# A two-layer hybrid block on one core: the rest of both layers' modulation on TensorE within the first mixers, instead of on GpSimd and ScalarE during the dense feed-forward

## The chip, the cores and the metric

The kernel runs on one core of one Trainium2 chip. The metric is device time in microseconds from the first to the last instruction of an execution, as the median of several runs. TensorE is called PE, its weight loads PEld, VectorE DVE, ScalarE ACT, GpSimd POOL; SP is the engine whose queue issues the transfers of this kernel.

## The reference

Two layers work on 256 latent and 256 context tokens of width 1024. Each layer first makes its modulation: six vectors of 1024 (shift, scale and gate for the mixers and for the feed-forward), once from the conditioning vector `c` and once from `c_ctx`. The two columns of silu(c) are multiplied with a 1024 x 6144 matrix per layer.

```python
for l in range(DEPTH):
    mod_lat = (jax.nn.silu(c) @ ada_w[l] + ada_b[l])[:, None, :]
    mod_ctx = (jax.nn.silu(c_ctx) @ ada_w[l] + ada_b[l])[None, None, :]
    sh_m, sc_m, g_m, sh_f, sc_f, g_f = jnp.split(mod_lat, N_MOD, axis=-1)
    hx = modulate(rmsnorm(x, norm_mix_g[l]), sh_m, sc_m)
    yx, _, _ = mix(l, hx @ w_in[l], True, hf_c[:, -1], hb_c[:, 0])
    x = x + g_m * yx
    hxf = modulate(rmsnorm(x, norm_ffn_g[l]), sh_f, sc_f)
    x = x + g_f * channel_mix(l, hxf)
```

`mix` splits the input projection into Fourier, Hyena and S5 heads and joins them with an output projection. `channel_mix` is a dense SwiGLU of width 2816 in the first layer and eight SwiGLU experts (two per token) in the second. The context tokens run through the first layer in the same way and through the second as far as the S5 states.

## The kernel before, in words

All operands are 32-bit; the large matmuls split each weight tile into a high part (`wh`, L189 on ScalarE) and a rest (`wl`, L190 on VectorE) and do three products (`mm3`). The kernel runs in stages: the start (modulation needed first, the norm, the Hyena filter and the S5 parameters of layer one), `mixers(0, ...)` (input projection in 14 tiles, S5 in six groups of four heads' groups, Hyena, Fourier), the output projection with residual and norm (L1156, L512 to L541), the dense feed-forward (gate and up into `pgu`, down into `pacc`, L1214 the residual), `mixers(1, ...)`, the router, and the experts, which stream 336 MB of weights.

The modulation has 48 columns of 128 per layer, kept in `mods[l]`; twelve chunks of four columns each. It is made in three ways. `ada_pe` (start, layer one's chunks 0 to 3) and `ada_ring` (chunks 4 to 7) use TensorE: a chunk's weights come as 512-wide rows, eight matmuls with the two columns of silu(c) as stationary operand write four strips of 32 partitions of one PSUM tile `pad`, ScalarE copies it to `adr`, four small matmuls with `sum4` add the strips up and transpose them, and ScalarE copies the result to `mods`. `ada_ring` reads a chunk in four transfers of 512 KB into a ring of two buffers `ar`. The third way is `ada` (L427): each of the other 64 columns comes transposed (`adaT`), and for each of the two vectors either VectorE multiplies and sums at once (L435, 8 times) or GpSimd multiplies with `crow`, a copy of silu(c) on all partitions (L438), and ScalarE sums (L439), 88 times. Columns 32 to 47 of layer one are made around the output projection, the 48 of layer two in `ahead(fi)`, eight per round of the feed-forward, with the layer's S5 matrices (`mats1`). `mods_done` adds the bias (L382) and makes the scale `Gm` (L385). `crow` itself is made at the start by 16 matmuls into `pcr`.

`fill0(q)` is called by `mixers` after S5 group q (0 to 5) and once at its end (6); it places the ring chunks. A scheduler orders the instructions of each engine; each engine then executes its own list strictly in that order, SP's list of transfers too, and waits on semaphores.

Of the kernel before, what the change touches and what calls it, by code (L numbers as in the profile page):

```python
# [8 lines left out]
F32 = mybir.dt.float32  # L9
# [71 lines left out]
def _prep(i):  # L81
# [6 lines left out]
    a['adaN'] = cc(i['ada_w'][0].reshape(KD, 128, 12, 512).transpose(2, 1, 0, 3))  # L88
    a['adaT'] = cc(i['ada_w'].transpose(0, 2, 1).reshape(2, 48, 128, D))
# [44 lines left out]
def build(tc, A, out, dbg=None, upto='all'):  # L134
# [71 lines left out]
    crow = par.tile([128, 2, D], F32, name="crow")  # L206
# [182 lines left out]
    def ada_pe(c, pool, cnt=[0]):  # L389
        pa = pt_('acc', (128, 512), "pad")  # L390
        for kh in range(2):
            cnt[0] += 1
            if cnt[0] % 2 or pool is None:
                r = load(A['adaN'][c][:, 4 * kh:4 * kh + 4], 4, 512)
            else:
                r = pool.tile([128, 4, 512], F32, name="raw2", tag="raw2", bufs=2)
                SP.dma_start(r, A['adaN'][c][:, 4 * kh:4 * kh + 4])
            for k in range(4):
                mm(pa[32 * k:32 * k + 32], scol32[:, 8 * kh + 2 * k:8 * kh + 2 * k + 32], r[:, k], kh == 0, kh == 1)
        row = (pool or wraw).tile([128, 512], F32, name="adr", tag="adr" if pool else "raw", bufs=1 if pool else 2)  # L400
        act(row, pa, AF.Copy)
        pt = pa[:, 0:8].rearrange("p (j s) -> p j s", s=2)
        for j in range(4):
            mm(pt[:, j], row[:, 128 * j:128 * j + 128], sum4, j == 0, j == 3, skip_group_check=True)
        act(mods[0][:, 4 * c:4 * c + 4], pt, AF.Copy)
        mods_done(0, 4 * c, 4)


    def ada_ring(c, pool):
        pa = pt_('acc', (128, 512), "pad")  # L410
        for j in range(4):
            r = pool.tile([128, 2, 512], F32, name="ar", tag="ar", bufs=2)
            SP.dma_start(r, A['adaN'][c][:, 2 * j:2 * j + 2])
            for i in range(2):
                k = 2 * j + i
                b = 32 * (k % 4)
                mm(pa[b:b + 32], scol32[:, 2 * k:2 * k + 32], r[:, i], j < 2, j > 1)
        row = pool.tile([128, 512], F32, name="adr", tag="ar", bufs=2)
        act(row, pa, AF.Copy)
        pt = pa[:, 0:8].rearrange("p (j s) -> p j s", s=2)  # L420
        for j in range(4):
            mm(pt[:, j], row[:, 128 * j:128 * j + 128], sum4, j == 0, j == 3, skip_group_check=True)
        act(mods[0][:, 4 * c:4 * c + 4], pt, AF.Copy)
        mods_done(0, 4 * c, 4)


    def ada(l, m0, m1, eng, pool):  # L427
        for m in range(m0, m1):
            r = pool.tile([128, D], F32, name="ar", tag="ar", bufs=2)
            SP.dma_start(r, A['adaT'][l, m])  # L430
            for s in range(1 if l == 1 and m >= 16 else 0, 2):
                o = mods[l][:, m, s:s + 1]
                if eng(m, s) == 'v':
                    jk = par.tile([128, D], mybir.dt.bfloat16, name="jk", tag="jk", bufs=1)
                    stt(jk, r, 1.0, crow[:, s], op0=mul, op1=mul, accum_out=o)  # L435
                else:
                    pd = par.tile([128, D], F32, name="pd", tag="pd", bufs=1)
                    gtt(pd, r, crow[:, s], op=mul)  # L438
                    act(pd, pd, AF.Copy, accum_out=o)  # L439
            if m % 8 == 7:  # L440
                mods_done(l, m - 7, 8, 1 if l == 1 and m >= 16 else 0)
# [108 lines left out]
    def s5_mats(p, l, q, M, rh, rd):  # L550
# [25 lines left out]
        for i, (src, op) in enumerate(((bre, sub), (bim, add))):  # L576
            tt_(src, bt(PB[0]), bh(bb[:, i]), op=mul)
            (tt_ if l else gtt)(x2, bt(PB[1]), bh(bb[:, 1 - i]), op=mul)
# [503 lines left out]
    with tc.tile_pool(name="filt", bufs=1) as p_:  # L1082
# [7 lines left out]
        with tc.tile_pool(name="prm", bufs=1) as p2_, tc.tile_pool(name="start", bufs=1) as st, banks(f=3, fk=1):  # L1090
# [3 lines left out]
            for s in range(2):  # L1094
                for h in range(2):
                    pb = paux((128, 4, 128), "pcr")
                    for k in range(4):
                        mm(pb[:, k], scol[:, 4 * h + k, s:s + 1].to_broadcast([128, 128]), ident, True, True)
                    act(crow[:, s, 512 * h:512 * h + 512], pb.rearrange("p a b -> p (a b)"), AF.Copy)
# [14 lines left out]
    with z_es:  # L1114
# [3 lines left out]
        with tc.tile_pool(name="z0p", bufs=1) as z2, tc.tile_pool(name="ada0", bufs=1) as p_:  # L1118
            def fill0(q):
                if q == 0:  # L1120
                    ada_ring(4, p_)
                if q == 1:
                    ada_ring(5, p_)
                if q == 3:
                    ada_ring(6, p_)
                if q == 4:
                    ada_ring(7, p_)
            mixers(0, hH, hL, z2, yH, yL, fill0)
# [13 lines left out]
        ada(0, 32, 36, lambda m, s: 'gv'[s], apl)  # L1142
        ada(0, 36, 40, lambda m, s: 'gv'[s], apl)
        ada(0, 40, 44, lambda m, s: 'gg'[s], apl)
        ada(0, 44, 48, lambda m, s: 'gg'[s], apl)
# [41 lines left out]
    with tc.tile_pool(name="ffn", bufs=2, side="right") as fp, banks(gu=3, fk=1):  # L1187
# [42 lines left out]
        def ahead(fi):  # L1230
            ada(1, 8 * fi, 8 * fi + 8, lambda m, s: 'g', apl)
            for q in MATS1[fi]:
                mats1(q)
# [584 lines left out]
```

## Time and profile before

| | |
|---|---|
| median of 3 runs | 1851.45 us (1850.5 to 1854.9) |
| profiled execution | 1846.75 us, its span 1844.9 us |
| PE busy | 1708.1 us (93%) |
| DVE, ACT, POOL busy | 824.4, 445.1, 535.0 us |
| moved by DMA | 506.83 MB, 275 GB/s in the mean |

The span is the profiled execution from its first to its last instruction. An engine's busy time counts its compute instructions; PE's matmuls are pipelined and their ends are modelled, so that a full PE need not be PE at its peak. Each instruction is named by its line in the kernel and by the tiles that it writes and reads; the idle time ahead of it is put down to what came last.

### The profile page before, as it was taken

Reading aid. Unit: us, or ns where it says so; the run is one execution under the profiler, and the core shown is the slowest. Engines: PE = TensorE matmul, PEld = TensorE weight load, DVE = VectorE, ACT = ScalarE, POOL = GpSimd, SP = SyncE. Lnnn points to the kernel's source line nnn. Section 1 sums busy time; section 2 is a strip of 40 time slices with the busy share of each in tenths; the row PEclk is TensorE's granted clock in tenths of the full one; section 3 lists DMA queues with packets and bytes.
Section 4 is the critical chain, followed back from the end, with each engine's and each line's share of the span. In section 5 each row is a group of like instructions: output and inputs, shape, how many; then the busy total and the mean of one; then the engine's idle time right before and its main releaser. Section 6 shows DMA issues by size and latency. Waiting matters only on the chain. (4 is left out here: it accounts for less than half of the span.)

```text
span 1844.9 us, 47520 instructions
## 1 busy us (share of the span) xinstructions
PE 1708.1 (93%) x20961; PEld 1195.9 (65%) x20961; DVE 824.4 (45%) x1506; ACT 445.1 (24%) x798; POOL 535.0 (29%) x546
## 2 busy tenths in 40 slices
PE   7988899899989999998898999999999989999984
PEld 3665667777667667778777666666666656666642
DVE  7589968875776767264963001110111101011102
ACT  3332324455444443234332000000000000000000
POOL 5965535567787666012420000000000000000000
PEclk7998999999999999999998999999999999999998
DMA  8243345434556565353839999999999999999993
GB/s 296 88 121 119 100 140 179 142 119 137 175 175 203 188 195 192 120 155 127 248 138 419 405 391 417 419 419 419 419 418 419 419 419 419 415 417 413 415 413 155
DMA packets 150728, 506.83 MB, mean 275 GB/s; under 512 B 18478, under 2 KB 78704, under 8 KB 106480
## 3 DMA queue, kind: packets, MB, share of 16 engines
q1 hardware_dynamic: 150512, 503.70, 71.7%
q8 instruction: 166, 2.72, 0.6%
q14 instruction: 50, 0.41, 0.1%
HBM read 489.34 MB, written 14.32 MB: 273 GB/s over the span
## 5 line engine op out<-in xcount | busy, mean ns | idle before, releaser
L146 PE MATMUL pgu<-raw,xe 128*32 128x256 f32 x9408 | 530.4, 379 | 12.3 <-DMA raw<-in_mwp_dram 11.2
L146 PEld LDWEIGHTS pgu<-raw,xe 128*32 128x32 f32 x9408 | 319.5, 110 | 207.9 <-DMA raw<-in_mwp_dram 15.4
L1639 DVE TENSOR_TENSOR sg<-sg,pgu 128x384 f32<-128x384 f32 (+1 forms) x56 | 28.2, 504 | 630.2 <-ACT sg L1638 630.2
L146 PE MATMUL py<-raw,hT 128*32 128x256 f32 x4704 | 271.5, 379 | 7.8 <-DMA raw<-in_mwp_dram 7.8
L1534 POOL TENSOR_TENSOR ob<-ob,fgb 128x512 f32<-128x512 f32 x1 | 1.3, 1261 | 880.5 <-ACT ob L1533 880.5
L438 POOL TENSOR_TENSOR pd<-ar,crow 128x1024 f32<-128x1024 f32 x88 | 223.7, 2542 | 106.9 <-ACT pd L439 84.9
L190 DVE TENSOR_TENSOR wl<-raw,wh 128x1024 fp32r<-128x1024 f32 x109 | 188.3, 1731 | 92.2 <-ACT wh L189 86.7
L146 PEld LDWEIGHTS py<-raw,hT 128*32 128x32 f32 x4704 | 157.8, 110 | 108.5 <-DMA raw<-in_mwp_dram 7.8
L1638 ACT ACTIVATE sg<-pgu 128x384 f32<-128x384 f32 (+1 forms) x56 | 25.2, 450 | 706.2 <-PE pgu L146 706.2
L189 ACT ACTIVATE wh<-raw 128x1024 fp32r<-128x1024 f32 x109 | 114.5, 1054 | 162.0 <-PE pacc L146 77.9
L146 PE MATMUL pgu<-fhL,wh 128*128 128x512 f32 (+1 forms) x376 | 146.0, 389 | 3.8 <-DVE fhL L541 3.8
L146 PE MATMUL pgu<-fhH,wh 128*128 128x512 f32 (+1 forms) x392 | 146.7, 385 | 1.4 <-ACT sg L1270 0.8
L146 PE MATMUL pgu<-fhH,wl 128*128 128x512 f32 (+1 forms) x360 | 143.0, 398 | 4.0 <-DVE wl L190 3.9
L439 ACT ACTIVATE pd<-pd 128x1024 f32<-128x1024 f32 x88 | 93.1, 1058 | 131.1 <-POOL pd L438 127.7
L146 PE MATMUL pacc<-hL,wh 128*128 128x256 f32 (+1 forms) x248 | 88.2, 357 | 2.9 <-POOL hL L500 2.3
L146 PE MATMUL pacc<-HH,wh 128*128 128x512 f32 (+1 forms) x192 | 76.9, 401 | 14.4 <-DVE xT L1214 11.8
L146 PE MATMUL pacc<-hH,wh 128*128 128x256 f32 (+1 forms) x248 | 86.6, 359 | 3.7 <-DVE hq L829 1.6
L146 PE MATMUL pacc<-hH,wl 128*128 128x256 f32 (+1 forms) x248 | 86.7, 351 | 1.7 <-DVE wl L190 1.7
L146 PEld LDWEIGHTS pgu<-fhL,wh 128*128 128x128 f32 x376 | 72.0, 191 | 21.4 <-DVE fhL L541 4.6
L146 PEld LDWEIGHTS pgu<-fhH,wh 128*128 128x128 f32 x392 | 73.9, 193 | 16.5 <-ACT sg L1270 1.0
L146 PEld LDWEIGHTS pgu<-fhH,wl 128*128 128x128 f32 x360 | 68.7, 191 | 23.8 <-DVE wl L190 5.3
L146 PE MATMUL pacc<-HL,wh 128*128 128x512 f32 (+1 forms) x192 | 74.6, 389 | 0.0
(591 smaller groups left out, 2446.4 us busy)
## 6 DMA issues: line engine op xcount, KB each, us to landing
raw<-in_mwp_dram SPq DMA_DIRECT2D x336, 1024.0 KB
ar<-in_adaT_dram SPq DMA_DIRECT2D x64, 512.0 KB
raw<-in_w_in_dram SPq DMA_DIRECT2D x14, 1024.0 KB
raw<-in_fwg_dram SPq DMA_DIRECT2D x11, 1024.0 KB
raw<-in_fwu_dram SPq DMA_DIRECT2D x11, 1024.0 KB
raw<-in_fwd_dram SPq DMA_DIRECT2D x11, 1024.0 KB
raw<-in_adaN_dram SPq DMA_DIRECT2D x8, 1024.0 KB
ar<-in_adaN_dram SPq DMA_DIRECT2D x16, 512.0 KB
```

The lines of the kernel that those rows point to most:

```text
L146: return PE.matmul(o, l, r, start=start, stop=stop, **kw)
L189: act(h, r, AF.Copy)
L190: tt_(l, r, h.bitcast(F32), op=sub)
L438: gtt(pd, r, crow[:, s], op=mul)
L439: act(pd, pd, AF.Copy, accum_out=o)
L1534: gtt(o_, o_, fgb[:, hs], op=mul)
L1638: act(sg[:, 0:n], p[:, 0:n, 0:128], AF.Silu)
L1639: tt_(sg[:, 0:n], sg[:, 0:n], p[:, 0:n, 128:256], op=mul)
```

## The change

`ada` and `crow` go, and with them all of GpSimd's products and ScalarE's sums. `ada_ring` takes a layer, and makes chunks 4 to 11 of layer one and all twelve of layer two, 20 instead of 4. `fill0` hands out two chunks after the first S5 group and three after each later one and at the end. The ring has three buffers, and `adr` one of its own. The weights of both layers now lie in DRAM as `adaN`; the bytes read stay the same. In `s5_mats`, the product `x2` of the second layer's matrices goes from VectorE to GpSimd, as in the first layer.

```diff
-    def ada_ring(c, pool):
+    def ada_ring(l, c, pool):
         pa = pt_('acc', (128, 512), "pad")
         for j in range(4):
-            r = pool.tile([128, 2, 512], F32, name="ar", tag="ar", bufs=2)
-            SP.dma_start(r, A['adaN'][c][:, 2 * j:2 * j + 2])
+            r = pool.tile([128, 2, 512], F32, name="ar", tag="ar", bufs=3)
+            SP.dma_start(r, A['adaN'][l, c][:, 2 * j:2 * j + 2])
             for i in range(2):
                 k = 2 * j + i
                 b = 32 * (k % 4)
                 mm(pa[b:b + 32], scol32[:, 2 * k:2 * k + 32], r[:, i], j < 2, j > 1)
-        row = pool.tile([128, 512], F32, name="adr", tag="ar", bufs=2)
+        row = pool.tile([128, 512], F32, name="adr", bufs=1)
         act(row, pa, AF.Copy)
         pt = pa[:, 0:8].rearrange("p (j s) -> p j s", s=2)
         for j in range(4):
             mm(pt[:, j], row[:, 128 * j:128 * j + 128], sum4, j == 0, j == 3, skip_group_check=True)
-        act(mods[0][:, 4 * c:4 * c + 4], pt, AF.Copy)
-        mods_done(0, 4 * c, 4)
-    def ada(l, m0, m1, eng, pool):
...
+        act(mods[l][:, 4 * c:4 * c + 4], pt, AF.Copy)
+        mods_done(l, 4 * c, 4)
@@ s5_mats
-            (tt_ if l else gtt)(x2, bt(PB[1]), bh(bb[:, 1 - i]), op=mul)
+            gtt(x2, bt(PB[1]), bh(bb[:, 1 - i]), op=mul)
@@ the start
-            for s in range(2):
-                for h in range(2):
-                    pb = paux((128, 4, 128), "pcr")
-                    for k in range(4):
-                        mm(pb[:, k], scol[:, 4 * h + k, s:s + 1].to_broadcast([128, 128]), ident, True, True)
-                    act(crow[:, s, 512 * h:512 * h + 512], pb.rearrange("p a b -> p (a b)"), AF.Copy)
@@ the first mixers
+            rest = [(0, c) for c in range(4, 12)] + [(1, c) for c in range(12)]
+
             def fill0(q):
-                if q == 0:
-                    ada_ring(4, p_)
...
+                for _ in range((2, 3, 3, 3, 3, 3, 3)[q]):
+                    ada_ring(*rest.pop(0), p_)
             mixers(0, hH, hL, z2, yH, yL, fill0)
@@ the output projection
-        ada(0, 32, 36, lambda m, s: 'gv'[s], apl)
-        ada(0, 36, 40, lambda m, s: 'gv'[s], apl)
-        ada(0, 40, 44, lambda m, s: 'gg'[s], apl)
-        ada(0, 44, 48, lambda m, s: 'gg'[s], apl)
@@ the dense feed-forward
         def ahead(fi):
-            ada(1, 8 * fi, 8 * fi + 8, lambda m, s: 'g', apl)
             for q in MATS1[fi]:
                 mats1(q)
```

How the scheduler places this is read from the two instruction lists (a count behind a row is of equal neighbours; line numbers of the change are a little lower, as `ada` is gone).

PE at the end of the first mixers, before: the Fourier step (`puab`, `pfn`) and Hyena's last products (`pj`), and then the output projection (`pacc<-yH`).

```order
L146 MATMUL puab<-bd,uf 128x256 x2
L146 MATMUL pj_2870<-ci,Yf 128x128 x5
L146 MATMUL puab<-bd,uf 128x256 x2
L146 MATMUL pj_2871<-ci,Yf 128x128 x5
L146 MATMUL pfn<-cl,uab 128x256 x8
L146 MATMUL pacc<-yH,wh 128x512 x2
```

PE at the same place in the change: the gate of S5 (`pglu`) and ring chunks (`pad<-ar` the weights, `pad<-sum_87` the small products) ahead of the output projection.

```order
L145 MATMUL pad<-ar,scol 32x512 x4
L145 MATMUL pglu<-ysT,gluw 128x512 x3
L145 MATMUL pad<-sum_87,adr 128x2 x4
L145 MATMUL pglu<-ysT,gluw 128x512 x3
L145 MATMUL pad<-ar,scol 32x512 x8
L145 MATMUL pad<-sum_87,adr 128x2 x4
L145 MATMUL pad<-ar,scol 32x512 x8
L145 MATMUL pad<-sum_87,adr 128x2 x4
L145 MATMUL pad<-ar,scol 32x512 x4
L145 MATMUL pacc<-yH,wh 128x512
```

Where nothing of the modulation stood, two and a half chunks now stand with nothing between them right ahead of the output projection, and the gate has moved among the chunks.

SP, the transfers from Hyena's second filter (`K`) to the output projection's weights, before: `ar<-in_adaT_dram` are the columns for GpSimd.

```order
L876 DMA K_2754<-kd_115 128x1536
L922 DMA gluw<-in_gluw_dram 128x1152
L198 DMA cd<-in_cd_dram 128x256
L198 DMA cl<-in_cl_dram 128x1024
L939 DMA fnw<-in_fnw_dram 128x128
L183 DMA raw<-in_w_out_dram 128x8x256
L430 DMA ar<-in_adaT_dram 128x1024 x2
L1136 DMA xT<-in_xT_dram 128x1024 x4
L430 DMA ar<-in_adaT_dram 128x1024 x2
L183 DMA raw<-in_w_out_dram 128x8x256
```

SP at the same place in the change:

```order
L411 DMA ar<-in_adaN_dram 128x1024 x12
L857 DMA K_3059<-kd_114 128x1536
L903 DMA gluw<-in_gluw_dram 128x1152
L197 DMA cd<-in_cd_dram 128x256
L197 DMA cl<-in_cl_dram 128x1024
L920 DMA fnw<-in_fnw_dram 128x128
L182 DMA raw<-in_w_out_dram 128x8x256
L411 DMA ar<-in_adaN_dram 128x1024 x15
L182 DMA raw<-in_w_out_dram 128x8x256
L411 DMA ar<-in_adaN_dram 128x1024 x12
L1107 DMA xT<-in_xT_dram 128x1024 x3
```

The second filter, the output weights and the residual stream `xT` now stand behind 12 to 39 ring transfers, each of which is issued only when PE has left the buffer that it overwrites.

GpSimd in the feed-forward around the first S5 matrices of layer two, before (`pd<-ar,crow` is the product of `ada`):

```order
L438 TENSOR_TENSOR pd<-ar,crow 128x1024 x2
L615 TENSOR_TENSOR M<-rotA,rotB 128x4x64 x2
L618 MEMSET rh 128x4
L438 TENSOR_TENSOR pd<-ar,crow 128x1024
L587 TENSOR_TENSOR M<-cs,PC_108 128x4x128
L588 TENSOR_TENSOR y_4765<-cs,PC_109 128x512
L562 TENSOR_TENSOR d_4749<-d_4749,id_92 128x16
L590 TENSOR_TENSOR M<-bb,PC_109 128x4x128
L438 TENSOR_TENSOR pd<-ar,crow 128x1024
```

And in the change:

```order
L596 TENSOR_TENSOR M<-rotA,rotB 128x4x64 x2
L599 MEMSET rh 128x4
L568 TENSOR_TENSOR M<-cs,PC_107 128x4x128
L569 TENSOR_TENSOR y_4892<-cs,PC_108 128x512
L543 TENSOR_TENSOR d_4876<-d_4876,id_91 128x16
L571 TENSOR_TENSOR M<-bb,PC_108 128x4x128
L599 MEMSET rh 128x4
L559 TENSOR_TENSOR x_4891<-PB_106,bb 128x512
```

The large products are gone, and `x_4891` is the product `x2` that VectorE made before.

## Rows read from the trace of the kernel before

**Rows 1.** The page's first part: busy us, share of the span, instructions.
```profile
PE 1708.1 (93%) x20961; PEld 1195.9 (65%) x20961; DVE 824.4 (45%) x1506; ACT 445.1 (24%) x798; POOL 535.0 (29%) x546
```

**Rows 2.** Windows: us, busy (count) of PE, PEld, DVE, ACT, POOL; clock, DMA, GB/s.
```profile
110.00:257.00 147.00, 128.96 (x1246) 89.03 (x1247) 125.55 (x274) 42.65 (x84) 69.81 (x81) 0.91 0.38 119
257.00:293.00 36.00, 35.64 (x163) 25.53 (x163) 23.69 (x42) 13.41 (x25) 17.68 (x17) 1.00 0.32 111
293.00:400.00 107.00, 92.79 (x562) 79.65 (x560) 96.43 (x135) 55.82 (x99) 59.38 (x24) 0.95 0.47 155
400.00:738.00 338.00, 315.05 (x1512) 239.10 (x1512) 235.04 (x258) 154.83 (x251) 248.38 (x151) 0.97 0.55 181
738.00:784.00 46.00, 46.00 (x212) 35.11 (x211) 12.94 (x14) 11.85 (x16) 1.70 (x2) 1.00 0.37 120
...
960.00:1845.00 885.00, 838.81 (x15100) 529.46 (x15098) 136.29 (x326) 57.38 (x125) 1.26 (x1) 0.98 0.98 402
```

**Rows 3.** Groups by line: GpSimd's products and ScalarE's sums; busy us, mean ns.
```profile
L438 POOL TENSOR_TENSOR pd<-ar,crow 128x1024 f32<-128x1024 f32 x88 | 223.7, 2542 | 106.9 <-ACT pd L439 84.9 <-DMA ar<-in_adaT_dram 22.0
L439 ACT ACTIVATE pd<-pd 128x1024 f32<-128x1024 f32 x88 | 93.1, 1058 | 131.1 <-POOL pd L438 127.7 <-POOL rh L618 3.2
```

**Rows 4.** VectorE's weight split: 400 to 738 (mean; then min/median/max ns), last 738 to 800.
```profile
L190 DVE TENSOR_TENSOR wl<-raw,wh 128x1024 fp32r<-128x1024 f32 x48 | 102.4, 2134 | 48.6 <-ACT wh L189 48.4
...
L190 DVE TENSOR_TENSOR wl<-raw,wh x48: 1208/2244/3419, 398.4 to 737.3; 128x1024 fp32r<-128x1024 f32 x48
...
L190 DVE TENSOR_TENSOR wl<-raw,wh x11: 1208/1226/1228, 737.3 to 797.3; 128x1024 fp32r<-128x1024 f32 x11
```

**Rows 5.** PE's waits, 400 to 738: us in total, times, longest.
```profile
PE pacc L146 <- DVE xT L1214: 11.8, 7, 3.7
PE pgu L146 <- DVE wl L190: 3.9, 2, 3.3
```

**Rows 6.** PE's waits, 293 to 400.
```profile
PE pacc L146 <- ACT nac L512: 4.1, 1, 4.1
```

**Rows 7.** PE's timeline in the mixers: start us, us, instruction.
```profile
236.21 0.39 PE L146 MATMUL pacc<-hH,wh 128*128 128x512 f32 x1
236.44 0.40 PE L146 MATMUL pacc<-hL,wh 128*128 128x512 f32 x1
236.77 1.05 PE L146 MATMUL pad<-ar,scol 128*32 128x512 f32 x4
237.75 0.50 PE L146 MATMUL pacc<-hH,wl 128*128 128x512 f32 x1
...
248.62 0.95 PE L146 MATMUL pad<-sum,adr 128*128 128x2 f32 x8
249.43 0.89 PE L146 MATMUL pU<-z,ce 128*128 128x384 f32 x2
...
292.78 0.81 PE L146 MATMUL pacc<-yH,wh 128*128 128x512 f32 x2
```

**Rows 8.** Windows: the start, while `adaN` is read.
```profile
10.00:20.00 10.00, 5.99 (x31) 2.25 (x30) 9.08 (x60) 2.90 (x4) 1.34 (x1) 0.73 1.00 413
```

**Rows 9.** Waits, 110 to 257 (GpSimd), and of SP's queue, 100 to 300.
```profile
POOL M L587 <- DMA cs<-in_s5c_dram: 14.8, 4, 6.0
...
SPq L413 <- PE pad L146: 12.7, 8, 3.6
```

**Rows 10.** PE's timeline at the start.
```profile
4.97 4.29 PE L146 MATMUL pcr<-ident,scol 128*128 128x128 f32 x24 [4.97 <-DMA fw<-in_fw_dram]
...
13.91 0.64 PE L146 MATMUL pad<-raw,scol 128*32 128x512 f32 x4 [3.00 <-DMA raw<-in_adaN_dram]
```

**Rows 11.** The line that ends a chunk of the modulation: min/median/max ns.
```profile
L382 DVE TENSOR_TENSOR mods<-mods,colp x16: 155/202/2334, 21.5 to 724.0; 128x8 f32<-128x8 f32 x12, 128x16 f32<-128x16 f32 x4
```

**Rows 12.** Groups by line: the product `x2`, on GpSimd and on VectorE.
```profile
L578 POOL TENSOR_TENSOR x<-PB,bb 128x512 f32<-128x512 f32 x12 | 15.0, 1246 | 6.5 <-DVE bre L579 3.2 <-DVE bb L246 2.5 <-DVE mods L382 0.8
L578 DVE TENSOR_TENSOR x<-PB,bb 128x512 f32<-128x512 f32 x12 | 11.3, 940 | 0.1
```

More of the change, by code (lines that the diff above doesn't have):

```diff
@@ L87, in _prep @@
     a['ccol'] = cc(np.stack([i['c_ctx'], i['c'][0]], 0).reshape(2, KD, 128).transpose(2, 1, 0))
-    a['adaN'] = cc(i['ada_w'][0].reshape(KD, 128, 12, 512).transpose(2, 1, 0, 3))
-    a['adaT'] = cc(i['ada_w'].transpose(0, 2, 1).reshape(2, 48, 128, D))
+    a['adaN'] = cc(i['ada_w'].reshape(2, KD, 128, 12, 512).transpose(0, 3, 2, 1, 4))
     def cols(v, n):
@@ L205, in build @@
     SP.dma_start(scol, A['ccol'])
-    crow = par.tile([128, 2, D], F32, name="crow")
     ident, sel = const(cst, 'ident'), const(pre, 'sel')
@@ L393, in ada_pe @@
             if cnt[0] % 2 or pool is None:
-                r = load(A['adaN'][c][:, 4 * kh:4 * kh + 4], 4, 512)
+                r = load(A['adaN'][0, c][:, 4 * kh:4 * kh + 4], 4, 512)
             else:
                 r = pool.tile([128, 4, 512], F32, name="raw2", tag="raw2", bufs=2)
-                SP.dma_start(r, A['adaN'][c][:, 4 * kh:4 * kh + 4])
+                SP.dma_start(r, A['adaN'][0, c][:, 4 * kh:4 * kh + 4])
             for k in range(4):
@@ L422, in ada_ring @@
             mm(pt[:, j], row[:, 128 * j:128 * j + 128], sum4, j == 0, j == 3, skip_group_check=True)
-        act(mods[0][:, 4 * c:4 * c + 4], pt, AF.Copy)
-        mods_done(0, 4 * c, 4)
-    def ada(l, m0, m1, eng, pool):
[L428 to L441, printed above, removed]
+        act(mods[l][:, 4 * c:4 * c + 4], pt, AF.Copy)
+        mods_done(l, 4 * c, 4)
     def rsqrt_small(ms, n, nm, tmp=tmp, e=V):
@@ L1118, in build @@
         with tc.tile_pool(name="z0p", bufs=1) as z2, tc.tile_pool(name="ada0", bufs=1) as p_:
+            rest = [(0, c) for c in range(4, 12)] + [(1, c) for c in range(12)]
             def fill0(q):
-                if q == 0:
-                    ada_ring(4, p_)
[L1122 to L1127, printed above, removed]
+                for _ in range((2, 3, 3, 3, 3, 3, 3)[q]):
+                    ada_ring(*rest.pop(0), p_)
             mixers(0, hH, hL, z2, yH, yL, fill0)
```

## The prediction

> **What bounds the kernel now.** I read the page's first part, then the windows by stage, then single stretches. TensorE (PE) is busy for 1708.1 us of a span of 1844.9 [rows 1]. From 960 us on the expert stage moves 402 GB/s with the DMA engines at 0.98 and TensorE at 838.8 of 885 us [rows 2]; the change touches nothing there, so that stage is only shifted, and what counts is how much earlier or later it begins.
>
> Ahead of it four stretches matter [rows 2]. First mixers up to the second Hyena step (110 to 257): PE 128.96 of 147 us, VectorE (DVE) 125.55, mean granted clock 0.91; two engines are nearly full, and they wait for each other. Mixers' tail (257 to 293): PE 35.64 of 36, clock 1.00, so PE alone sets it. Output projection and norm (293 to 400): PE 92.79 of 107, DVE 96.43. Dense feed-forward (400 to 738): PE 315.05 of 338, clock 0.97, GpSimd 248. When GpSimd falls silent (738 to 784) PE is busy for all 46.00 us at clock 1.00.
>
> **What the change removes.** GpSimd loses 88 products (2.54 us each, 223.7 us) and ScalarE the 88 sums over them (93.1 us) [rows 3]. Neither engine bounds anything there, so this pays only through what they hold up. The reader is to see it in the weight split on DVE (L190): 48 of them take 2.13 us in the mean while GpSimd multiplies, and 1.21 to 1.23 us each once it has stopped [rows 4]. 48 x 0.9 = 43 us of DVE time goes, yet DVE has 235 of 338 us busy, so that too pays only where PE waits. Those waits between 400 and 738 are 11.8 + 3.9 us and smaller ones [rows 5], of 22.95 us of PE idle time in all (338 - 315.05). To idle time comes the lower clock: a mean of 0.97 between 1.2 and 2.4 GHz is 6% of 338 us, or 20 us, at half speed, 10 us lost at most. Between 293 and 400 the same sums give 14.2 idle and 5.3 for the clock, with waits for a norm that ScalarE delivers late (4.1, the longest) [rows 6] and smaller ones.
> Lower end: only the waits named on L190 and half of those on L1214 and L512 go, about 12 us. Upper end: both stretches run as 738 to 784 does, 33 (22.95 + 10) + 19.5 (14.2 + 5.3) = 52 us. I take two thirds of the 33 and half of the 19.5, since the norm's chain stays as it is: **-32 us**. What is late next is the norm's chain and the filter's and the scan matrices' own DVE steps.
>
> **What it adds.** Sixteen chunks more of `ada_ring`, in the mixers and the first output tiles. In PE's order the weight matmuls on `ar` form 64 groups (up to four neighbours on different column strips) where there were 14, because most stand in pairs between other work. A pair holds PE for 0.98 us (236.77 to 237.75), and the four small products with `sum4` for 0.81 (248.62 to 249.43) [rows 7]. The trace counts each of these matmuls twice (x4 for a pair). 50 groups x 0.98 = 49.0, 16 x 0.81 = 13.0: **+62 us** of PE work at the full clock.
> By place: 24 groups and 6 sums ahead of the second Hyena step (28.4 us), 24 and 9 from there to the first output matmul (30.8 us), 2 and 1 in the output projection (2.8 us). The second and third lie where PE is full (35.64 of 36), so they are paid whole. For the first there is a cover: 18 us of PE idle time between 110 and 257, plus at most 13 us from the clock (0.91: 18% of 147 us at half speed). Ends: nothing hidden, or all 28.4. PE's holes there come from waits for DVE, and a ring matmul fits into a hole only where the order has put it; I let it hide the idle time and no more: **-18 us**. If that cover is gone, these 18 us come back.
> Two projection tiles also move from ahead of the second Hyena step to behind it; that shifts work between two stretches and adds none.
>
> **DMA and the SP queue.** 32 MB are read either way, as 64 transfers of 512 KB; they now come between 110 and 350 us. The engines moved 413 GB/s with such blocks early on [rows 8], 1.27 us a tile; the tail's 34 tiles then need 43 us beside 31 of ring work and some 47 of other matmuls (the 36 of before and the two tiles, 24 matmuls each, one every 0.23 us: 236.21 to 236.44 [rows 7]), so bandwidth does not bind on the whole. It does at the end: ten tiles stand almost alone ahead of the output projection, 12.7 us by the queue against 5 x 0.98 + 2 x 0.81 = 6.5 us of PE, and PE waits for ScalarE's copy of each chunk. SP also issues in order: a ring transfer waits until PE has left its buffer, and loads behind it wait too. Already now GpSimd sat 14.8 us over four waits for the small `cs` loads that were late, and SP 12.7 us on ring buffers [rows 9]. No row shows ten chunks where four stood; the nearest are these. Ends 0 and 25 us; I take **+8 us**, the 6 us at the end and a little ahead of it.
>
> **Small edits.** `pcr` leaves PE's start (4.29 us for 24 of its 32), but PE then waits 3.00 us for `adaN` data at 13.91 [rows 10]: worth nothing, the transfer is the cover. `mods_done` runs 24 times instead of 16, at 0.2 us on DVE [rows 11], and all 16 that are new or moved now stand in the mixers; in a stretch where DVE has 125 of 147 us I charge **+2**.
> The product `x2` of the second layer's scan matrices goes from DVE (12 x 0.94) to GpSimd (1.25 each where it already runs there) [rows 12]; both then have room, and I count nothing; ends -5 and +5. The Trainium skill ("SBUF — State Buffer", Who interferes with whom) speaks against this move: a DVE instruction with two SBUF inputs and a GpSimd instruction that reads SBUF exclude each other for their whole length. The trace agrees, with the split at up to 3.42 us against 1.21 alone [rows 4]. By that rule the 12 products cost DVE up to 15 us of blocking for 11.3 us of work saved; PE would see at most a few of these.
>
> **Sum.** 62 - 18 + 8 + 2 - 32 = **+22 us**. The profiled execution took 1846.75 us (span 1844.9), so it would take 1869; the median of the runs is 1851.45, 4.7 above it, and the forecast is for the median: 1873.5 us.
>
> **Rivals.**
> *The mixers swallow it (faster).* PE's busy time ahead of 257 us may hold more room than it shows. Weight loads fill 89.03 of 147 us (0.61) there, and 35.11 of 46 (0.76) where PE certainly is full [rows 2]: 147 x (1 - 0.61/0.76) = 29 us of room, so all 28.4 hide; with the feed-forward at its upper end the sum is 62 - 28 + 2 - 48 = -12, so 1839 us. It decides once hidden ring work and recovered waits exceed 64 us together; I have 50. For it: every L190 after 738 ran at the short time. Against it: DVE is as full as PE in that stretch. The Trainium skill ("Perfetto Trace Analysis", Identifying the Most-Contended Engine) holds matmul busy time to be a bad measure of PE's headroom and asks for the share of weight loads; no row here tells which of the two measures is right, and by the rule the sum would be 10 us lower.
> *The SP queue (slower still).* The small loads for `s5_mats` stand behind ring transfers, DVE starves in the one stretch that it helps to bound. With 5 us a group (the longest of those waits was 6.0) for five of the six groups, and nothing hidden: 62 + 25 + 2 - 32 = +57, so 1908 us. It decides once such waits reach DVE. For it: they are there with 4 chunks, where 10 now stand. Against: the ring has three buffers instead of two.
> *A wash.* Both reliefs larger than I take them, -28 and -40: 62 - 28 + 8 + 2 - 40 = +4 us, 1855.
>
> **Chances.** My forecast (some +8 to +45) 0.50, the wash 0.13, the SP queue 0.13, the faster rival 0.24. A measurement here tells about 0.3%, 5.5 us, from no change. Faster 0.24, same 0.12, slower 0.64. The range reaches to the faster rival at its likeliest and to the SP rival: 1837 to 1908; the forecast's own is 1859 to 1896.
>
> **What would show it.** Right: the first output matmul, now at 292.8 [rows 7], later by 45 to 55 us; L190 at 1.2 to 1.3 us in the whole feed-forward; PE idle there under 10 us; the stretch from there to 960 shorter by about 30. Wrong: a first output matmul less than 35 us later (ring work hidden), or PE waits on `ar` of over 25 us (queue), or a feed-forward whose waits stay although DVE is fast (they were not GpSimd's doing).

## The result, and the profile after

The kernel after the change takes 1895.84 us in the median (1891.86 to 1897.48, 4 runs) against 1851.12 us before (1850.5 to 1854.9, 4 runs): ratio 1.0241, 95% interval 1.0226 to 1.0257, or 44.7 us slower. The forecast said slower, by 22 us, with 1837 to 1908 as its range: the sign holds, and the forecast size is half of what came.

The profiled execution took 1897.09 us (span 1895.2), 50.3 us more than that of before (1846.75, span 1844.9). The page's first part answers to [rows 1]:

```profile
PE 1765.2 (93%) x21313; PEld 1212.4 (64%) x21313; DVE 711.8 (38%) x1489; ACT 359.9 (19%) x650; POOL 323.3 (17%) x470
```

GpSimd is 212 us less busy and ScalarE 85, as the removed products and sums would have it. To see where 50 us came from, I cut both spans at the same instructions: the first transpose of an S5 group (`pbt`), the first matmul of the second Hyena step (`pU<-z`), the first and last output matmul and the last gate matmul. The columns are those of [rows 2]. Before:

```profile
0.00:107.70 107.70, 90.97 (x393) 58.51 (x393) 72.14 (x216) 40.48 (x70) 82.86 (x188) 0.84 0.50 171
107.70:241.90 134.20, 115.73 (x1189) 80.11 (x1189) 118.27 (x258) 41.66 (x81) 65.90 (x77) 0.90 0.43 134
241.90:292.80 50.90, 50.54 (x259) 35.65 (x259) 33.21 (x60) 15.21 (x29) 23.53 (x23) 1.00 0.24 83
292.80:353.10 60.30, 52.30 (x334) 46.55 (x333) 55.23 (x74) 28.38 (x51) 34.16 (x13) 0.94 0.52 172
353.10:783.40 430.30, 401.13 (x1950) 306.98 (x1949) 289.20 (x333) 193.91 (x313) 275.50 (x162) 0.97 0.52 170
```

After:

```profile
0.00:110.90 110.90, 84.75 (x360) 53.98 (x360) 69.70 (x216) 38.21 (x66) 82.70 (x188) 0.86 0.48 165
110.90:247.60 136.70, 117.84 (x1191) 73.77 (x1191) 100.06 (x225) 38.47 (x79) 65.70 (x75) 0.84 0.61 188
247.60:387.00 139.40, 125.29 (x627) 67.90 (x625) 58.54 (x121) 36.29 (x67) 25.06 (x25) 0.94 0.70 235
387.00:439.40 52.40, 52.32 (x352) 46.47 (x349) 21.16 (x54) 12.36 (x27) 0.00 (x0) 0.97 0.13 40
439.40:835.20 395.80, 388.86 (x1950) 299.42 (x1949) 206.01 (x307) 109.00 (x157) 96.75 (x98) 1.00 0.36 114
```

| stretch | before | after | difference |
|---|---|---|---|
| start | 107.7 | 110.9 | +3.2 |
| mixers, up to the first output matmul | 185.1 | 276.1 | +91.0 |
| output projection | 60.3 | 52.4 | -7.9 |
| dense feed-forward | 430.3 | 395.8 | -34.5 |
| all behind it | 1061.5 | 1060.0 | -1.5 |

The feed-forward does what the change is about. In it PE now idles for 6.9 us where it idled for 29.2, the clock stands at 1.00, and VectorE's weight split runs at the short time, 1.23 us at the median, where it had 2.24 [rows 4]:

```profile
L189 DVE TENSOR_TENSOR wl<-raw,wh x58: 1203/1226/2079, 461.6 to 830.5; 128x1024 fp32r<-128x1024 f32 x58
```

The mixers pay more than twice that. Of the 91.0 us, 76.9 are PE's busy time (166.27 to 243.13) and 14.1 its idle time (18.83 to 32.96). Nearly all of the busy time is the ring's own: its weight matmuls and sums (`pad`, PE's busy time and clock in the same two stretches) take 21.45 us before and 96.63 after, 75.2 more. Before, then after:

```profile
107.70:241.90 134.20, 19.45 (x84) 0.90 0.43 134
241.90:292.80 50.90, 2.00 (x12) 1.00 0.24 83
```
```profile
110.90:247.60 136.70, 42.19 (x184) 0.84 0.61 188
247.60:387.00 139.40, 54.44 (x280) 0.94 0.70 235
```

Much of the idle time lies at the very end; here are the matmuls ahead of the first output matmul (PE's timeline: start us, us, instruction, idle time and what ended it):

```profile
366.96 1.05 PE L145 MATMUL pad<-ar,scol 128*32 128x512 f32 x4 [2.85 <-DMA ar<-in_adaN_dram]
368.71 1.38 PE L145 MATMUL pad<-sum,adr 128*128 128x2 f32 x8 [0.70 <-ACT adr L417]
370.02 1.94 PE L145 MATMUL pad<-ar,scol 128*32 128x512 f32 x8
375.08 1.92 PE L145 MATMUL pad<-ar,scol 128*32 128x512 f32 x4 [3.12 <-DMA ar<-in_adaN_dram]
380.65 1.92 PE L145 MATMUL pad<-ar,scol 128*32 128x512 f32 x4 [3.64 <-DMA ar<-in_adaN_dram]
383.33 1.87 PE L145 MATMUL pad<-sum,adr 128*128 128x2 f32 x8 [0.76 <-ACT adr L417]
385.13 1.94 PE L145 MATMUL pad<-ar,scol 128*32 128x512 f32 x8
387.00 0.79 PE L145 MATMUL pacc<-yH,wh 128*128 128x512 f32 x1
```

In PE's list nothing else stands there, so it waits for tiles, and behind the waits the clock falls: a pair of matmuls takes 1.05 us at 366.96 and 1.92 at 375.08. One window shows that end, with 352 GB/s and a granted clock of 0.60 in the mean:

```profile
365.00:387.00 22.00, 11.82 (x45) 4.02 (x45) 6.00 (x9) 4.97 (x8) 0.00 (x0) 0.60 0.95 352
```

The ring's tiles do not have the DMA engines, 0.95 busy, to themselves there. Of the 6.5 MB whose transfers were issued in this window 2.5 are ring tiles; the residual stream and two weight tiles come with them:

```profile
ar<-in_adaN_dram SPq DMA_DIRECT2D x5, 512.0 KB
xT<-in_xT_dram SPq DMA_DIRECT2D x4, 512.0 KB
raw<-in_w_out_dram SPq DMA_DIRECT2D x1, 1024.0 KB
raw<-in_fwg_dram SPq DMA_DIRECT2D x1, 1024.0 KB
```

How much of the waits this sharing makes, and how much the short ring, the experiments separate only in part (e8).

The waits of SP's queue show the other side: a ring transfer may be issued only once PE has left its buffer. On `ar` SP stood 12.7 us over 8 waits before [rows 9], and now:

```profile
SPq L411 <- PE pad L145: 141.4, 56, 10.5
```

Loads behind such a wait are late. GpSimd waits 26.9 us for the small `cs` where it was 14.8 [rows 9], and PE 7.1 us, where it was 2.8, for an S5 matrix that is read back from DRAM (from 110 to 263 us; waited for: us in total, times, longest):

```profile
POOL M L568 <- DMA cs<-in_s5c_dram: 26.9, 5, 9.4
...
PE py L145 <- DMA M<-rd: 7.1, 2, 4.2
```

### The profile page after: what moved, and what is told of

Read it like the earlier page. It is cut to its first block, busy times and chain, and to the rows that moved or that the text cites. A ratio compares the mean times of both kernels' runs of the same rounds, so it can differ in the third digit from the quotient of the medians.

```text
span 1895.2 us, 47950 instructions
## 1 busy us (share of the span) xinstructions
PE 1765.2 (93%) x21313; PEld 1212.4 (64%) x21313; DVE 711.8 (38%) x1489; ACT 359.9 (19%) x650; POOL 323.3 (17%) x470
## 5 line engine op out<-in xcount | busy, mean ns | idle before, releaser
L189 DVE TENSOR_TENSOR wl<-raw,wh 128x1024 fp32r<-128x1024 f32 x109 | 142.3, 1308 | 140.1 <-ACT wh L188 135.1
L145 PE MATMUL pad<-ar,scol 128*32 128x512 f32 x320 | 76.7, 670 | 11.7 <-DMA ar<-in_adaN_dram 11.6
L145 PE MATMUL pacc<-HH,wl 128*128 128x512 f32 (+1 forms) x192 | 71.5, 378 | 0.3 <-DVE wl L189 0.3
```

The costliest lines, as they stand in the source:

```text
L145: return PE.matmul(o, l, r, start=start, stop=stop, **kw)
L189: tt_(l, r, h.bitcast(F32), op=sub)
```

## The experiments

Two questions: what the sixteen chunks pay for in the mixers, and what the feed-forward gains by. Each kernel ran beside the kernel before on the same chip; its medians there were 1851.3, 1851.5 and 1849.0 us.

**e1_noprod and e2_nodma: GpSimd's products, or the transfers?** Both edit the kernel before, in `ada` for layer two.

```diff
             SP.dma_start(r, A['adaT'][l, m])
+            if l:
+                act(mods[l][:, m], r[:, 0:2], AF.Copy)
...
+                continue
```

> The kernel before, with the 56 products of the second layer's modulation on GpSimd and their 56 sums on ScalarE left out (two numbers of each tile are copied in their place, so the second layer's modulation is not the reference's), the 48 transfers of 512 KB kept. If GpSimd's products held the dense feed-forward up (theory), the feed-forward from its first matmul to its last drops from 430 us to about 396, as in the kernel after, and the time to about 1817 us. If the 24 MB of transfers held it up (rival), it stays over 420 us and the time over 1840.

(There are 64 such products, not 56.) Measured: 1832.65 us, ratio 0.9902 (0.9878 to 0.9926); feed-forward 418 us.

```diff
+            if l and m >= 2:
+                r = kept[m % 2]
+            else:
                 r = pool.tile([128, D], F32, name="ar", tag="ar", bufs=2)
                 SP.dma_start(r, A['adaT'][l, m])
...
```

> The kernel before, with 46 of the 48 transfers of 512 KB of the second layer's modulation left out and every product and sum kept, on the two tiles that are loaded (so the second layer's modulation is not the reference's). Theory (GpSimd's products hold the feed-forward up): the feed-forward stays over 420 us, the time over 1843. Rival (the transfers do): about 396 us and 1817.

Measured: 1842.56 us, ratio 0.9954 (0.9936 to 0.9972); feed-forward 426 us. Neither theory has it all: products and sums bring 12 us of the feed-forward's 34, the transfers 5. The first layer's columns, still there in both, weigh on the start of the stretch (e3). The split itself does not depend on the transfers: its median from 400 to 730 us is 1.23 us without the products and 2.56 with them and without the transfers. e1 takes GpSimd's products and ScalarE's sums away together; the timeline of the kernel before (400 to 738) tells them apart. The four splits that ran beside a sum and nothing on GpSimd took 1.21 to 1.23 us, the 30 beside a product 1.32 to 3.42. A short split is not enough, though: in e1 PE is still idle for 20.1 us of the stretch. First e1, then e2:

```profile
L190 DVE TENSOR_TENSOR wl<-raw,wh x48: 1210/1226/3174, 406.1 to 728.0; 128x1024 fp32r<-128x1024 f32 x48
```
```profile
L190 DVE TENSOR_TENSOR wl<-raw,wh x46: 1210/2556/3421, 406.3 to 726.2; 128x1024 fp32r<-128x1024 f32 x46
```

**e3_half: half of the change.** The kernel after, with the second layer's `ada`, `crow` and `pcr` put back, and the ring as in the kernel before: two buffers, with `adr` in them.

```diff
-            rest = [(0, c) for c in range(4, 12)] + [(1, c) for c in range(12)]
+            rest = [(0, c) for c in range(4, 12)]
...
-                for _ in range((2, 3, 3, 3, 3, 3, 3)[q]):
+                for _ in range((2, 1, 1, 1, 1, 1, 1)[q]):
...
         def ahead(fi):
+            ada(1, 8 * fi, 8 * fi + 8, lambda m, s: 'g', apl)
```

> Half of the change: the first layer's last four chunks on TensorE in the mixers, the second layer's modulation on GpSimd in the feed-forward as in the kernel before (ring of two buffers, as before). Theory (each chunk costs TensorE its own 4.7 us, four groups of 0.98 and one of 0.81, and nothing of it is hidden; the rest of the 94 us is starvation and lower clock at the end, which this kernel hardly has): first output matmul 19 to 25 us later than in the kernel before, at 312 to 318; output projection 8 us shorter; feed-forward unchanged at 430; time about 1863 us. Rival (up to some amount the work is hidden and only the sixteen chunks together overrun): first output matmul under 303, time 1848 or less.

Measured: 1844.06 us, ratio 0.9962 (0.9946 to 0.9979), a gain. First output matmul at 306.2 us, output projection 52.2, feed-forward 420.7. Its mixers, cut as above:

```profile
108.50:239.20 130.70, 111.11 (x1184) 75.53 (x1184) 112.10 (x236) 41.90 (x81) 69.15 (x77) 0.92 0.48 150
239.20:306.20 67.00, 66.77 (x353) 42.32 (x352) 47.74 (x89) 20.30 (x39) 28.43 (x25) 1.00 0.55 189
```

The first four new chunks cost 13.4 us, 3.4 each, and give back 8 us in the output projection and 10 in the feed-forward. So the first layer's four chunks are worth moving. The other twelve are not: they put the first output matmul off by another 80.8 us (2.4 of them at the start), 6.7 each, and give back some 25 us in the feed-forward. (The ring differs between the two kernels as well.)

**e9_after_nodma: eleven of the second layer's twelve chunks without their transfers.** The kernel after:

```diff
+            if l and c:
+                r = kept[j % 3]
+            else:
                 r = pool.tile([128, 2, 512], F32, name="ar", tag="ar", bufs=3)
                 SP.dma_start(r, A['adaN'][l, c][:, 2 * j:2 * j + 2])
...
```

> The kernel after, with 44 of the 48 transfers of the second layer's chunks left out: its twelve chunks multiply tiles that are loaded already (so the second layer's modulation is not the reference's), with all their matmuls, copies and sums. Theory (of the 81 us by which the twelve chunks make the first output matmul later than in e3_half, TensorE's own work is 12 x 4.7 = 56, and some 25 are tiles that come late, a ring that is too short, and the lower clock behind such waits): first output matmul at 355 to 369 us, time about 1872 us. Rival (all 81 us are TensorE's work and its interleaving with the mixers, whatever the transfers do): 380 or later, time 1888 or more.

Measured: 1867.38 us, ratio to before 1.0088 (1.007 to 1.0106); first output matmul at 357.0. The theory holds: 30 of the 80.8 us hang on the transfers, some 51 (4.2 a chunk) are left when the tiles are there. A single profiled execution tells this to a few us only: in e10, whose PE list is the same as in the kernel after up to the first output matmul and which ran beside e9, that matmul stands at 381.0 and not at 387.0, so 24 us behind e9's. In the medians e9 is 28.5 us faster than the kernel after. The end of the mixers, at clock 0.98 and with 2.9 us of PE idle time where the kernel after had 14.1:

```profile
110.70:244.70 134.00, 114.29 (x1191) 71.86 (x1191) 102.24 (x224) 38.37 (x79) 66.05 (x74) 0.87 0.61 191
244.70:357.00 112.30, 109.44 (x635) 66.76 (x633) 57.04 (x119) 33.83 (x66) 26.16 (x25) 0.98 0.25 82
```

**e8_ring4: a longer ring.** The kernel after with `bufs=4` for `ar`.

> The kernel after with four ring buffers instead of three. Theory (the waits for tiles at the end of the mixers and SP's waits for buffers come from a ring that is too short to read ahead): TensorE's wait for tiles between 263 us and the first output matmul falls from 11.6 to under 6 us, the clock at the end rises from 0.60, the time falls by 6 to 12 us, to 1884-1890. Rival (the last tiles are bound by the transfers themselves, 512 KB each at some 350 GB/s behind the output weights): within 4 us of the kernel after, 1892 or more.

Measured: 1875.28 us, ratio 1.0128 (1.0109 to 1.0146), 20.6 us better than the kernel after, about twice what I expected. First output matmul at 369.3, 17.7 us earlier; PE's wait for tiles from 254 us to there 4.2 us; SP's waits on PE fall from 141.4 to 112.0 us:

```profile
111.00:254.10 143.10, 125.79 (x1241) 78.20 (x1238) 110.04 (x241) 43.19 (x88) 65.98 (x76) 0.88 0.65 204
254.10:369.30 115.20, 106.51 (x572) 58.74 (x571) 51.19 (x102) 29.75 (x57) 24.16 (x23) 0.98 0.68 239
```
```profile
PE pad L145 <- DMA ar<-in_adaN_dram: 4.2, 3, 3.6
...
SPq L411 <- PE pad L145: 112.0, 48, 9.8
```

PE's idle time in the mixers falls by 7 us (33.0 to 26.0) and its busy time by 11: the clock is higher (0.88 and 0.98 against 0.84 and 0.94), and more pairs stand together, four of them in 1.92 us. The profiled executions differ by 17.1 us; the rest of the 20.6 is the runs' scatter. So the waits were owed to the ring's length in good part, although the residual stream and an output weight tile still came among the last tiles (350 to 370 us).

**e4_quad: fours instead of pairs.**

```diff
-        for j in range(4):
-            r = pool.tile([128, 2, 512], F32, name="ar", tag="ar", bufs=3)
-            SP.dma_start(r, A['adaN'][l, c][:, 2 * j:2 * j + 2])
-            for i in range(2):
+        for j in range(2):
+            r = pool.tile([128, 4, 512], F32, name="ar", tag="ar", bufs=2)
+            SP.dma_start(r, A['adaN'][l, c][:, 4 * j:4 * j + 4])
+            for i in range(4):
...
```

> The kernel after, with each chunk read as two tiles of 1 MB instead of four of 512 KB, and four matmuls on the four column strips one behind the other where two stood. Theory (a group holds TensorE about 1 us whether it has two matmuls or four): 20 chunks have 40 groups instead of 80, so up to 39 us less; with some of the old groups already merged I expect 25 to 35 us less, 1862 to 1870 us, and TensorE's waits for the tiles between 263 and the first output matmul up from 12 to some 20 us. Rival (the matmuls of a group don't share the time, the engine is held by the number of matmuls or by the transfers): within 10 us of the kernel after, 1886 or more.

Measured: 1878.65 us, ratio 1.0147 (1.0129 to 1.0166): 17 us less than the kernel after, short of the 25 expected and above the rival's 10. Ring work and sums keep PE busy for 72.2 us instead of 99.75, so four matmuls do share their time; but two tiles of 1 MB are also a longer ring than three of 512 KB, as long as e8's, so the gain in time is not the groups' alone. And the clock at the end is lower (0.91 against 0.94) and the waits for tiles remain (8.6 us, and 3.6 for ScalarE's copy). Part of what fours save goes back into waiting.

**e10_x2dve: the product `x2` back on VectorE.**

```diff
-            gtt(x2, bt(PB[1]), bh(bb[:, 1 - i]), op=mul)
+            (tt_ if l else gtt)(x2, bt(PB[1]), bh(bb[:, 1 - i]), op=mul)
```

> The kernel after, with the product x2 of the second layer's scan matrices back on VectorE. I counted this edit at nothing, with ends of -5 and +5 us: time within 5 us of the kernel after's 1895.8. By the Trainium skill (SBUF — State Buffer, Who interferes with whom) the move to GpSimd can cost VectorE up to 15 us of blocking in the feed-forward; if TensorE sees most of it, this kernel is 8 us or more faster, at 1888 or less.

Measured: 1896.90 us (1892.54 to 1900.73), ratio to before 1.0255 (1.0235 to 1.0275); against the kernel after (1.0241) no difference. The blocking is there, in the sum that follows the product (L560, `bim`, six in the feed-forward): 679 ns at the median in this kernel and 1110 with `x2` on GpSimd. But it touches few instructions, and PE has only 6.9 us of idle time in the whole stretch of the kernel after.

**e11_late: the second layer's chunks on TensorE in the feed-forward.** As e3_half without `ada`, with groups of four from three buffers of 512 KB, and

```diff
         def ahead(fi):
+            for c in (2 * fi, 2 * fi + 1):
+                ada_ring(1, c, apl)
```

> The first layer's last chunks on TensorE in the mixers as in the kernel after, the second layer's twelve on TensorE too, but in the feed-forward, two at each of its six steps; groups of four throughout. Theory (what the second layer's chunks cost in the mixers beyond TensorE's own time is owed to the place; in the feed-forward the engine is never idle and the clock is 1.00): each costs two groups of 0.98 and one of 0.81 to 0.95, so the feed-forward goes from 396 to 396 + 12 x 2.9 = 431 us, and the time is 302.8 (first output matmul of e6_half_quad) + 50 + 431 + 1060 + 2 = about 1846 us. Rival (a chunk stalls TensorE wherever it is put, by its copy on ScalarE and its tiles): feed-forward 450 or more, time over 1862.

Measured: 1881.17 us, ratio 1.0167 (1.0151 to 1.0183): a miss by 35 us: 19 more in the first mixers, 21 more behind the feed-forward (1080.9 us instead of 1060), a little less between. The feed-forward took 428.9 us at full clock, near the 431 expected, but with ten of the twelve chunks in it, so 3.3 us each; the other two, 10.66 us of PE time, slipped behind it into the second layer's mixers. And the first mixers took longer than those of e6_half_quad below, with the same eight chunks: first output matmul at 321.7 against 302.8. That e11 has no `pcr` at the start, like the kernel after, may have a part in it; it was not tried.

**e5, e6, e7 and e12: what e3_half still lacked.** e5_half_v makes the second layer's products on VectorE, as one multiply-and-sum each; e6_half_quad puts e3's ring matmuls in fours; e7 does both.

```diff
-            ada(1, 8 * fi, 8 * fi + 8, lambda m, s: 'g', apl)
+            ada(1, 8 * fi, 8 * fi + 8, lambda m, s: 'v', apl)
```

> The half change (e3_half), with the second layer's 64 products and sums made on VectorE, each as one multiply-and-sum of 1.21 us, instead of on GpSimd and ScalarE. Theory (what holds the feed-forward up is GpSimd's long instructions, which stretch VectorE's; VectorE's own 64 x 1.21 = 78 us fit into its idle time): the weight split falls to a mean of 1.23 us, the feed-forward from 420 to 400-408 us, the time from 1844 to about 1829. Rival (TensorE waits on VectorE's queue, and a product in it costs as much there as a stretched split): feed-forward 418 or more, time 1842 or more.

> The half change (e3_half), with its eight chunks' matmuls in groups of four on the four column strips (three buffers of 512 KB). Theory (TensorE pays for each group, 0.98 us, and there are 16 fewer): first output matmul 10 to 15 us earlier than in e3_half (306.2), at 291 to 296, time about 1832 us. Rival (with eight chunks the groups stand in TensorE's idle time anyway, or two tiles come too late for a group of four): 301 or later, 1839 or more.

> Both together: groups of four in the mixers, the second layer's products on VectorE. If both theories hold, their gains lie in different stretches and add: 1844 - 12 - 15 = about 1817 us, faster than both kernels. If the rival of e5 holds, about 1830; if that of e6, about 1825; if both, about 1842.

Measured: e5 1836.79 us, ratio 0.9921 (0.9903 to 0.994), between its theory and its rival; e6 1840.49, 0.995 (0.9934 to 0.9966), first output matmul at 302.8, so 3.4 us earlier and not 10 to 15; e7 1833.80, 0.9912 (0.9895 to 0.993). The scheduler did not keep e6's fours together: most of its groups stand as six matmuls and two, so the edit saved few of them, and the result is the rival's. In e5 the feed-forward takes 409 us, close to what was expected, but the norm ahead of it grew: in e7 the first gate matmul stands 8.7 us behind the last output matmul. VectorE's timeline shows why. The scheduler has put the products as early as their data come, and each small step of the norm (`ny`, `nt`, 0.15 us) waits behind one of 1.2 us:

```profile
351.75 1.22 DVE L436 SCALAR_TENSOR_TENSOR jk<-ar,crow 128x1024 bf16<-128x1024 f32 x1
352.89 0.08 DVE L436 DVE_READ_ACCUMULATOR jk<-ar,crow 128x1 f32 x1
352.89 0.15 DVE L461 SCALAR_TENSOR_TENSOR nt<-nt,nv 128x2 f32<-128x2 f32 x1
352.96 1.22 DVE L1243 TENSOR_TENSOR wh<-raw,wh 128x1024 fp32r<-128x1024 f32 x1
354.10 1.22 DVE L436 SCALAR_TENSOR_TENSOR jk<-ar,crow 128x1024 bf16<-128x1024 f32 x1
355.24 0.08 DVE L436 DVE_READ_ACCUMULATOR jk<-ar,crow 128x1 f32 x1
355.24 0.15 DVE L462 SCALAR_TENSOR_TENSOR ny<-nt,ny 128x2 f32<-128x2 f32 x1
```

So e12_paced calls `ada` behind each of the feed-forward's 22 tiles and lets `jk`, the product that is written beside its sum and read by nobody, share the rotating buffers of the gate tiles, which ties it to them (no run separates these two edits):

```diff
-            ada(1, 8 * fi, 8 * fi + 8, lambda m, s: 'v', apl)
...
+                    t = f0 + c + m
+                    ada(1, 48 * t // nff, 48 * (t + 1) // nff, lambda m, s: 'v', apl)
...
-                    jk = par.tile([128, D], mybir.dt.bfloat16, name="jk", tag="jk", bufs=1)
+                    jk = tmp.tile([128, D], mybir.dt.bfloat16, name="jk", tag="t512a", bufs=2)
```

> The kernel of e7_half_quad_v, with the second layer's products on VectorE spread over the feed-forward's 22 tiles (two or three behind each) instead of as early as their data come. Theory (in e7 the products stood in VectorE's queue between the steps of the norm ahead of the feed-forward, so its first matmul came 8.7 us after the last output matmul, where e3_half has 0.3): that gap falls under 2 us, the time to about 1826 us. Rival (VectorE's 78 us cost the same wherever they stand): 1831 or more.

Measured: 1814.01 us (1810.51 to 1817.66), ratio 0.980 (0.9782 to 0.9819): the fastest of all, 35 us under the kernel before and 82 under the kernel after. The gap is gone (output matmuls end and gate matmuls begin at 349.8), and the feed-forward itself came down to 402.7 us, beyond what I expected:

```profile
302.00:349.80 47.80, 47.80 (x334) 44.52 (x333) 27.16 (x59) 17.22 (x31) 0.00 (x0) 1.00 0.28 93
349.80:752.50 402.70, 392.85 (x1958) 303.69 (x1957) 282.79 (x443) 109.58 (x158) 103.11 (x98) 0.99 0.51 172
```
```profile
L436 DVE SCALAR_TENSOR_TENSOR jk<-ar,crow 128x1024 bf16<-128x1024 f32 x64 | 83.6, 1309 | 4.4 <-DMA ar<-in_adaT_dram 4.2
```

The 64 products cost VectorE 83.6 us, and the stretch is only 7 us longer than in the kernel after, which has none. Not all of the 35 us is their doing: e6, which has the same mixers and the products on GpSimd, stood at a ratio of 0.995, so the move to VectorE and the even spread together are worth some 27 us.

## Why the prediction was right in sign and short in size

Of the signs that I named, a split of 1.2 to 1.3 us, PE idle for under 10 us and a shorter feed-forward came. One did not: the first output matmul stands 94.2 us later, at 387.0, and not 45 to 55. PE's waits on `ar` (11.6 us from 110 to 400) stayed under the 25 that I named for the queue.

**The relief (-32 us): right, and too small.** It came to 42.4 us (7.9 and 34.5). The mechanism stands: the split at 1.23 us, PE idle for 6.9 us (I named under 10), the clock at 1.00. I took 32 us of a room of 52; it gave 42. What I had read from the split alone is more: in e1 the split is short and the feed-forward is 12 us shorter, not 34. The transfers bring 5 (e2), and taking the first layer's columns out of the output projection 10 (e3). These three are 27 us; where the rest of the 34.5 comes from stays open.

**The added work (+62 us): right at full clock.** Here is the account of the mixers' 91.0 us. Sixteen chunks less the two or three groups in the output projection are 59 us at full clock by my prices. The trace has 75.2 us more of ring work, at the granted clock. The clock accounts for the 16 us between, by an estimate from its means: a mean of 0.90 over 134.2 us is 26.8 us at 1.2 GHz; 0.84 over 136.7 and 0.94 over 139.4 are 60.5 us. That is 33.6 us more at half speed, at most 17 us lost. The idle time adds 14.1. Together 90. Why the clock was lower already ahead of the second Hyena step (0.84 against 0.90) no run separates.

**What hides it (-18 us): this step failed.** "I let it hide the idle time and no more": it hid nothing on balance. PE's idle time up to the second Hyena step was 18.5 us and is 18.9, though three input projection tiles left that stretch (I had counted two). My reason, that PE's holes there come from waits for VectorE, was half the matter: of 18.2 us of waits between 110 and 257 before, 10.5 were for VectorE, 4.9 for ScalarE and 2.8 for a transfer. That nothing was hidden shows with most of the transfers gone, too: in e9 the sixteen chunks put the first output matmul off by 64.2 us, 3.0 at the start and 61.2 in the mixers, and its ring work there, 80.8 us, is 59.3 more than before. The first four found hardly any cover either: e3 paid 13.4 us, and its ring work, 35.6 us, is 14.1 more than before (its expectation had charged 18.8). PE's busy time in `pad` in the mixers, first e3, then e9:

```profile
108.50:239.20 130.70, 24.26 (x120) 0.92 0.48 150
239.20:306.20 67.00, 11.32 (x66) 1.00 0.55 189
```
```profile
110.70:244.70 134.00, 40.06 (x184) 0.87 0.61 191
244.70:357.00 112.30, 40.69 (x288) 0.98 0.25 82
```

The faster rival fell by this too: it read 29 us of room from the weight loads' share of busy time. The Trainium skill ("Perfetto Trace Analysis", Identifying the Most-Contended Engine) trusts that share more than matmul busy time, beside a share of peak work that these profiles do not show; in this stretch the busy time was the better guide, since the work that was added found none of those 29 us.

**Transfers and queue (+8 us): the mechanism right, the size wrong.** e9 measures 24 to 30 us for the tiles of the second layer, in the 14.1 us of idle time and in the clock. I had priced the end at 6 us, as ten tiles' transfer time beside their matmuls at full speed. In the trace it is 22 us long: tiles a few us apart, behind and beside 4 MB of other loads that I had not counted, and from 370 us on the matmuls at half speed. That a wait also costs the clock behind it was in none of my terms; I had the clock only as a possible gain. Of the rival on SP's queue half came true. The `cs` waits grew from 14.8 to 26.9 us, but VectorE did not become the bound; PE itself waited, for tiles and for an S5 matrix. The ring, where "three buffers instead of two" spoke against it, was the weak point: one buffer more gave back 20.6 us.

**Small edits.** Taking `pcr` away was to be worth nothing, and it was: the first matmul of the input projection stands at 57.66 us and stood at 57.93, with 6.2 us less PE work in the start; the load of `fw` (PE's first wait, to 8.27 us) and a VectorE step (4.7 us) were its cover, and not `adaN`. The start's 3.2 us more come behind that, where PE's wait for GpSimd's `hL` grew from 2.3 to 4.7 us; why was not tried, and in e10 the start is 1.1 us shorter with the same PE list. The +2 for `mods_done` no run shows by itself. `x2` at nothing holds within the scatter (e10). The Trainium skill's rule of two engines that shut each other out ("SBUF — State Buffer", Who interferes with whom) shows in the rows of L560, but the up to 15 us of blocking that I had worked out with it did not reach TensorE: e10 was not faster.

So 62 - 18 + 8 + 2 - 32 should have read 59 + 17 + 14 + 3 - 42 - 1.5 = 50 in the profiled executions; in the medians 44.7. That 1895.84 still lies in my forecast's own range, 0.2 us from its end at 1896, is luck: a relief 10 us larger than I took it made up for part of the cover that was not there and of the late tiles.

## What to carry to other kernels

Here work that was moved onto the engine that sets the time paid its full price, and more where its data came through a short ring: price the wait, the clock behind it, and the loads that stand in the same queue behind it. Before moving work off a disturbing engine, ask whether a third one, with idle time in that stretch, can take it in shorter instructions; here one multiply-and-sum on VectorE in place of the second layer's products on GpSimd and sums on ScalarE, spread evenly, gained some 27 us, and 35 with the first layer's last four chunks on TensorE; the move of everything to TensorE lost 45. Look in the final order for where a scheduler puts such filler work: as early as its data allow is also in between the steps of a latency chain.

## What the runs showed of the hardware

Four matmuls of 32 columns on four column strips keep PE busy for hardly longer than two: a group of four stands at 1.06 us where a pair has 1.05, in the kernel after:

```profile
341.18 1.06 PE L145 MATMUL pad<-ar,scol 128*32 128x512 f32 x8
344.10 1.05 PE L145 MATMUL pad<-ar,scol 128*32 128x512 f32 x4
```

(Each matmul is counted twice.) And the granted clock fell in a stretch in which PE had work listed all the time and waited for its data: from 365 to 387 us it was busy for 11.82 of 22 us, at a mean clock of 0.60. In e9, where most of those tiles were there, the stretch from the second Hyena step to the first output matmul stands at 0.98.
